# The S5 scan's tile laid out by place in eight instead of chunk by chunk

## The chip, the cores and the metric

The kernel runs on one core of a Trainium2 chip. The metric is the device time of one execution in microseconds; the median of several executions counts. Beside it stands one execution recorded by the hardware profiler, from which all durations below are read. TensorE is called PE there, VectorE DVE, ScalarE ACT, GpSimd POOL, and SyncE, which issues most DMAs, SP.

## The reference, cut to what matters

One layer of a streaming encoder: two groups of heads side by side, latent attention and a diagonal state-space layer (S5), then a gated convolutional FFN. It is computed for a prompt of 1024 positions and for 8 running streams of 16 positions each. Only the S5 part is touched:

```python
bu_re = jnp.einsum('gpc,bsgc->bsgp', bb_re, ug)      # 32 groups, 64 complex states each
bu_im = jnp.einsum('gpc,bsgc->bsgp', bb_im, ug)
ar, ai, sr, si = lax.associative_scan(comb, (la_re, la_im, bu_re, bu_im), axis=1)
if h0_re is not None:                                 # running streams: carried state
    h_re, h_im = h0_re[:, None], h0_im[:, None]
    sr, si = sr + ar * h_re - ai * h_im, si + ar * h_im + ai * h_re
y = (jnp.einsum('gcp,bsgp->bsgc', p["s5_c_re"], sr)
     - jnp.einsum('gcp,bsgp->bsgc', p["s5_c_im"], si))
```

That is a linear recurrence s(t) = a s(t-1) + B u(t) for each of 32 x 64 complex states, and an output read from each state. Its last states are outputs too.

## The kernel before

All three phases of the kernel work on 1152 positions: 1024 of the prompt and 128 of the streams. `phase_a` norms and projects the input: first the S5 channels (`upart`), then for each 128 positions the query and kv latents (`natpart`, matmuls into `nat`). `phase_b` does the attention of the streams and the S5 layer, `phase_de` drives the prompt's attention (`phase_c`), the output projection and the FFN, which is most of the time.

The S5 layer cuts positions into chunks of 8 (`LC`), so there are 144 chunks (`NCH`): 128 of the prompt (`NPC`), then two for each of the 8 streams. `tables` computes powers of a and three sets of matrices: `Et` (from a chunk's input to its contribution to the state), `f_dram` (from a state to a chunk's outputs) and `kt_dram` (within a chunk). The last two are made by the generator `rest` in eight rounds, each with three VectorE operations of 128x576 (`tmpF`, `fo`), eight matmuls `kp`, a ScalarE copy into `kts`, one small VectorE addition and two stores.

`s5_states` (L424) computes each chunk's contribution: 32 groups, three to a PSUM bank `pst`, one matmul each (128 partitions: 64 real parts, 64 imaginary parts). ScalarE copies the real half into `RE` (L435), VectorE the imaginary half into `IM` (L436). Both are halves of the tile `RI`, [128, 2, 16, 144]: the partition is (half of the groups, state), then real or imaginary, then 16 groups, then the 144 chunks in order.

`s5_scan` (L438) makes of these the state at each chunk's end. The 128 chunks of the prompt are read as 16 blocks b of 8 places i, chunk = 8 b + i.
- Local steps, L474: for i = 1 to 7, `cmac2` adds a times place i-1 to place i, in all 16 blocks and 16 groups at once. One `cmac2` (L387) is five VectorE operations: a product of 512 elements, two of 256 with the other part and a sign, and two sums of 512. The works `v1` and `v2` (shown as `w`) are whole runs; the operands in `RI` step 8 elements, 32 bytes, within a group.
- Across blocks, L477 to 489: the last place of each block (`SL`) goes into `SB`, where small operations carry the states through four quarters (`SC`).
- Fix-up, L498 to 511: each block's places 0 to 6 get a's power times the state before the block, by `cmac` (L403: eight VectorE operations), four blocks at a time, 448 elements an operation. After each, ScalarE copies the states into `SP`, shifted by one chunk, for the output matmul: for each of real and imaginary and each half of the groups one copy of 64x448 and one of 64x64 from `SB`, 32 in all.
- Streams, L512 to 526: two `cmac` of 128 elements with the carried state `h0`, copies into `SP`, and the last states into `fin`.

`SP` is [128, 32, 144] in the order of chunks, since `s5_out` (L529) multiplies it and `U`, the input in chunks, by `Ft` and `Tt` into `py`.

`b8_open` and `b8_q` prepare the attention of the streams: loads of `cq`, `wq`, `wk`, `wkT` and small vectors, transposes `tq` with ScalarE copies `cqT`, projections, their sums of squares, and from them the factors `rrq`, `ex`; `b0` in `phase_b` goes on from there (`qah`, `qal`).

The order of the code is not the order on the chip. L1722 opens the tile context with `schedule_with_timeline_sim=True`: a planner orders each engine's instructions, SyncE's DMAs among them, by its own estimate of when each can start, apart from the stretches with a manual order (L1593). So the scan's steps, called in `phase_b` by `steps`, stand on VectorE between the work of `rest` and of `natpart`. Within an engine instructions run in the planned order. `GD` and `GF` are 16, so `cmac` and `cmac2` run on VectorE alone.

Of the kernel before, what the change touches and what calls it, by code (L numbers as in the profile page):

```python
# [75 lines left out]
def build(tc, t):  # L76
# [4 lines left out]
    with root:  # L81
# [19 lines left out]
        def acopy(out, in_, scale=1.0):  # L101
            nc.scalar.activation(out=out, in_=in_, func=AF.Copy, scale=scale)  # L102
# [321 lines left out]
        def s5_states():  # L424
            RI, h0, Et, U = [s5t[x] for x in ("RI", "h0", "Et", "U")]
            RE, IM = RI[:, 0], RI[:, 1]
            load(h0, t["h0"])
            for gh in range(2):
                for q0 in range(0, 16, 3):
                    n = min(3, 16 - q0)  # L430
                    p_ = psum("u", [P, n, NCH], "pst")
                    for g in range(n):
                        gg_ = gh * 16 + q0 + g
                        nc.tensor.matmul(p_[:, g], lhsT=Et[:, gg_], rhs=U[:, gg_], start=True, stop=True)
                    acopy(RE[64 * gh:64 * gh + 64, q0:q0 + n], p_[0:64])  # L435
                    nc.vector.tensor_copy(out=IM[64 * gh:64 * gh + 64, q0:q0 + n], in_=p_[64:P])  # L436

        def s5_scan():  # L438
            RI, SG, w1, PWr, PWi, SB, h0, fin, SC, QWr, QWi = [s5t[x] for x in (
                "RI", "SG", "w1", "PWr", "PWi", "SB", "h0", "fin", "SC", "QWr", "QWi")]  # L440
            RE, IM, SBr, SBi = RI[:, 0], RI[:, 1], SB[:, 0], SB[:, 1]
            nc.vector.tensor_copy(out=PWr[:, :, 0], in_=LRc)
            nc.vector.tensor_copy(out=PWi[:, :, 0], in_=LIc)

            def powers(xr, xi, n):
                d = 1
                while d < n:
                    ar, ai = xr[:, :, 0:d], xi[:, :, 0:d]
                    br = xr[:, :, d - 1:d].to_broadcast([P, 16, d])
                    bi = xi[:, :, d - 1:d].to_broadcast([P, 16, d])  # L450
                    orr, oi = xr[:, :, d:2 * d], xi[:, :, d:2 * d]
                    w = w1[:, :, 0:d]
                    mul(orr, ar, br)
                    mul(w, ai, bi)
                    sub(orr, orr, w)
                    mul(oi, ar, bi)
                    mul(w, ai, br)
                    add(oi, oi, w)
                    d *= 2

            powers(PWr, PWi, LC)
            nc.vector.tensor_copy(out=QWr[:, :, 0], in_=PWr[:, :, LC - 1])
            nc.vector.tensor_copy(out=QWi[:, :, 0], in_=PWi[:, :, LC - 1])
            powers(QWr, QWi, 4)
            for k, z in enumerate((PWi[:, :, 0], QWi[:, :, 0], QWi[:, :, 3])):
                ts(SG[:, k, 0], z, -1.0, None, ALU.mult)
                nc.vector.tensor_copy(out=SG[:, k, 1], in_=z)
            nc.vector.memset(SB[:, :, :, 0:1], 0.0)
            nc.vector.memset(SC[:, :, :, 0:1], 0.0)
            yield  # L470
            RP = RE[:, :, 0:NPC].rearrange("p g (b i) -> p g b i", i=LC)
            IP = IM[:, :, 0:NPC].rearrange("p g (b i) -> p g b i", i=LC)
            RIp = RI[:, :, :, 0:NPC].rearrange("p r g (b i) -> p r g b i", i=LC)
            for i in range(1, LC):  # L474
                cmac2(RIp[:, :, :, :, i], RIp[:, :, :, :, i - 1], RIp[:, :, :, :, i], 0, 16, GD)
                yield
            SL = RIp[:, :, :, :, LC - 1].rearrange("p r g (q n) -> p r g q n", n=4)  # L477
            SQ = SB[:, :, :, 1:17].rearrange("p r g (q n) -> p r g q n", n=4)
            nc.vector.tensor_copy(out=SQ[:, :, :, :, 0], in_=SL[:, :, :, :, 0])
            for i in range(1, 4):  # L480
                cmac2(SQ[:, :, :, :, i], SQ[:, :, :, :, i - 1], SL[:, :, :, :, i], 1, 4, 16)
            yield
            for q in range(4):
                cmac2(SC[:, :, :, q + 1:q + 2], SC[:, :, :, q:q + 1], SQ[:, :, :, q:q + 1, 3], 2, 1, 16)
            yield
            nc.vector.tensor_copy(out=SQ[:, :, :, :, 3], in_=SC[:, :, :, 1:5])
            qr, qi = [x[:, :, 0:3].rearrange("p g (o i) -> p g o i", o=1).to_broadcast([P, 16, 3, 3]) for x in (QWr, QWi)]
            cr_, ci_ = [SC[:, r, :, 1:4].rearrange("p g (b o) -> p g b o", o=1).to_broadcast([P, 16, 3, 3]) for r in range(2)]
            cmac(SQ[:, 0, :, 1:4, 0:3], SQ[:, 1, :, 1:4, 0:3], qr, qi, cr_, ci_, gd=16)
            yield  # L490
            SP = s5t["SP"] = s5t["pool"].tile([P, G, NCH], F32, tag="ES", name="SP")

            def sp_views(ri, gh):
                si = slice(64 * gh, 64 * gh + 64)
                o = SP[64 * ri:64 * ri + 64, 16 * gh:16 * gh + 16]
                return si, o[:, :, 0:NPC].rearrange("p g (b i) -> p g b i", i=LC), o[:, :, NPC:NCH].rearrange("p g (b i) -> p g b i", i=2)

            n7 = LC - 1  # L498
            pr = PWr[:, :, 0:n7].rearrange("p g (o i) -> p g o i", o=1).to_broadcast([P, 16, 4, n7])
            pi = PWi[:, :, 0:n7].rearrange("p g (o i) -> p g o i", o=1).to_broadcast([P, 16, 4, n7])  # L500
            for b0_ in range(0, 16, 4):
                bs_ = slice(b0_, b0_ + 4)
                br = SBr[:, :, bs_].rearrange("p g (b o) -> p g b o", o=1).to_broadcast([P, 16, 4, n7])
                bi = SBi[:, :, bs_].rearrange("p g (b o) -> p g b o", o=1).to_broadcast([P, 16, 4, n7])
                cmac(RP[:, :, bs_, 0:n7], IP[:, :, bs_, 0:n7], pr, pi, br, bi, gd=GF)
                for ri in range(2):
                    for gh in range(2):
                        si, ov, _ = sp_views(ri, gh)
                        acopy(ov[:, :, bs_, 1:LC], (RP, IP)[ri][si, :, bs_, 0:LC - 1])
                        acopy(ov[:, :, bs_, 0], SB[si, ri, :, bs_])  # L510
                yield
            RS = RE[:, :, NPC:NCH].rearrange("p g (b i) -> p g b i", i=2)  # L512
            IS = IM[:, :, NPC:NCH].rearrange("p g (b i) -> p g b i", i=2)
            m8r = PWr[:, :, 0:1].to_broadcast([P, 16, NB])
            m8i = PWi[:, :, 0:1].to_broadcast([P, 16, NB])
            cmac(RS[:, :, :, 0], IS[:, :, :, 0], m8r, m8i, h0[:, 0], h0[:, 1])
            cmac(fin[:, 0, :, 1:], fin[:, 1, :, 1:], m8r, m8i, RS[:, :, :, 0], IS[:, :, :, 0],
                 RS[:, :, :, 1], IS[:, :, :, 1])
            for ri in range(2):
                for gh in range(2):  # L520
                    si, _, os_ = sp_views(ri, gh)
                    acopy(os_[:, :, :, 0], h0[si, ri])
                    acopy(os_[:, :, :, 1], (RS, IS)[ri][si, :, :, 0])
            nc.vector.tensor_copy(out=fin[:, 0, :, 0], in_=SBr[:, :, 16])
            nc.vector.tensor_copy(out=fin[:, 1, :, 0], in_=SBi[:, :, 16])
            store(t["s5"], fin)
            yield
# [1216 lines left out]
```

## Time and profile before

| what | us |
|---|---|
| median of 3 runs | 1547.39 (1546.98 to 1550.94) |
| the profiled execution's own time | 1547.78 |
| its span, from the first to the last instruction | 1546.0 |
| TensorE busy | 1470.7 |
| VectorE busy | 1101.9 |
| ScalarE busy | 692.8 |

The S5 states are copied between 110.9 and 125.9 us, the scan runs from 125.9 to 226.7 us; all that is later than some 280 us has nothing of the change in it. A line of the timeline gives start, length, engine, line, operation and what it writes and reads, and in brackets the idle time of the engine before it and who ended it. A line of the groups gives the count, the busy time of all and the mean of one in ns. L105 is the line of a helper, so many groups have it; the tile names tell them apart.

### The profile page before, as it was taken

The page shows a single profiled execution, that of the slowest core. Times are in us where ns is not written, and L with a number is a line of the kernel's source. Part 1 is how long each engine was busy: PE and PEld are TensorE (multiplying, and loading weights), DVE is VectorE, ACT ScalarE, POOL GpSimd, SP SyncE. Part 2 cuts the span into 40 slices and gives each one's busy share as a digit, 9 for nine tenths or more (in the row PEclk, how much of TensorE's full clock was granted, in tenths as well). Part 3 has the DMA queues.
Part 4 walks back from the last instruction along what each step waited for, and adds up shares of the span by engine and source line. Part 5 has one row for each costly group of instructions (what it writes and reads, how often), then busy time and mean ns, then how long its engine had stood idle before and what let it go on. Part 6 is the DMA issues. An engine that isn't in the chain of part 4 may idle for free.

```text
span 1546.0 us, 23671 instructions
## 1 busy us (share of the span) xinstructions
PE 1470.7 (95%) x8733; PEld 1416.0 (92%) x8733; DVE 1101.9 (71%) x2317; ACT 692.8 (45%) x1351; POOL 261.8 (17%) x517
## 2 busy tenths in 40 slices
PE   6989759899899999999999999999999999999998
PEld 6988548787788999999999999999999999999998
DVE  8779986573878865567677766677777766777666
ACT  7444557575567876345233333333333333333321
POOL 3025222210635221112100000000000000000000
PEclk9999869999899999999999999999999999999999
DMA  7432553733211323630121111111111111111103
GB/s 204 113 128 74 167 154 70 233 78 97 79 58 58 103 67 101 199 88 15 41 68 43 42 44 48 47 41 42 42 42 41 42 42 42 42 42 42 42 1 133
DMA packets 92036, 117.95 MB, mean 76 GB/s; under 512 B 39060, under 2 KB 72980, under 8 KB 91188
## 3 DMA queue, kind: packets, MB, share of 16 engines
q1 hardware_dynamic: 91536, 116.25, 25.3%
q8 instruction: 68, 1.11, 0.3%
q14 instruction: 48, 0.39, 0.1%
q0 software_dynamic: 384, 0.20, 0.1%
HBM read 91.86 MB, written 24.56 MB: 75 GB/s over the span
## 4 chain that ended last, share of the span: by engine, by line
PE 77%; DVE 8%; ACT 2%; DMA 2%; issue 1%; SPq 0%; POOL 0%; DVEq 0%; ACTq 0%
PE pu L138 36%; PE pd L138 17%; PE pw L138 7%; PE pk L138 3%; PE pg L138 1%; DVE w L105 1%; PE pq L138 1%; PE po L1273 1%; PE pst L1261 1%; PE pst L1260 1%; PE pst L1262 1%; PE po L1271 1%; PE po L1272 1%; PE pZ L1032 1%; PE psm L1228 1%
## 5 line engine op out<-in xcount | busy, mean ns | idle before, releaser
L105 DVE TENSOR_TENSOR hT<-hT,pd 128x384 f32<-128x384 f32 x528 | 288.2, 551 | 217.6 <-PE pd L138 217.4
L138 PE MATMUL pu<-hnh,wh 128*128 128x384 f32 x1056 | 356.6, 338 | 0.0
L138 PE MATMUL pu<-hnl,wh 128*128 128x384 f32 x1056 | 356.4, 338 | 0.0
L138 PE MATMUL pu<-hnh,wl 128*128 128x384 f32 x1056 | 356.1, 337 | 0.0
L138 PE MATMUL pd<-act,wh 128*128 128x384 f32 x1056 | 348.7, 336 | 0.5 <-DVE hT L105 0.4
L1543 ACT ACTIVATE c<-pu,cvh 128x384 f32<-128x384 f32 x132 | 88.6, 671 | 308.8 <-PE pu L138 308.6
L138 PEld LDWEIGHTS pd<-act,wh 128*128 128x128 f32 x1056 | 197.7, 188 | 2.3 <-DVE hT L105 2.3
L138 PEld LDWEIGHTS pu<-hnh,wh 128*128 128x128 f32 x1056 | 198.4, 188 | 0.0
L138 PEld LDWEIGHTS pu<-hnl,wh 128*128 128x128 f32 x1056 | 198.3, 188 | 0.0
L138 PEld LDWEIGHTS pu<-hnh,wl 128*128 128x128 f32 x1056 | 198.0, 188 | 0.0
L123 DVE SCALAR_TENSOR_TENSOR c<-u,cvh,c 128x256 f32<-128x256 f32 (+1 forms) x352 | 171.2, 516 | 27.5 <-ACT u L102 14.2
L138 PE MATMUL pd<-act,wl 128*128 128x384 f32 x528 | 177.4, 336 | 0.0
L102 ACT ACTIVATE act<-c 128x384 fp32r<-128x384 f32 x66 | 34.7, 525 | 158.2 <-DVE c L105 158.2
L138 PEld LDWEIGHTS pd<-act,wl 128*128 128x128 f32 x528 | 99.2, 188 | 0.0
L105 DVE TENSOR_TENSOR wl<-ws,wh 128x1024 fp32r<-128x1024 f32 x74 | 92.0, 1248 | 8.0 <-ACT wh L102 8.0
L1549 POOL COPY u<-u 128x2 f32<-128x2 f32 x88 | 19.8, 225 | 384.3 <-DVE c L105 174.0
L102 ACT ACTIVATE wh<-ws 128x1024 fp32r<-128x1024 f32 x74 | 77.9, 1057 | 13.6 <-PE pw L138 7.5
L1565 ACT ACTIVATE c<-c 128x384 f32<-128x384 f32 x66 | 34.7, 525 | 75.5 <-DVE c L123 75.4
L1561 POOL COPY cvo<-u 128x2 f32<-128x2 f32 x44 | 8.1, 184 | 356.1 <-ACT u L102 356.1
L102 ACT ACTIVATE u<-pu 128x384 f32<-128x384 f32 (+2 forms) x176 | 66.3, 404 | 0.0
L138 PE MATMUL pw<-oh,wh 128*128 128x384 f32 x192 | 65.1, 340 | 0.2 <-DVE ql L123 0.2
L138 PE MATMUL pw<-oh,wl 128*128 128x384 f32 x192 | 64.4, 336 | 0.0
(450 smaller groups left out, 3043.1 us busy)
## 6 DMA issues: line engine op xcount, KB each, us to landing
ws<-in_w_up SPq DMA_DIRECT2D x44, 512.0 KB, 3.5
ws<-in_w_down SPq DMA_DIRECT2D x22, 512.0 KB, 3.6
xs<-in_xT SPq DMA_DIRECT2D x24, 192.0 KB, 3.0
os<-o_dram SPq DMA_DIRECT2D x24, 192.0 KB, 2.8
hT<-in_xT SPq DMA_DIRECT2D x24, 192.0 KB, 4.6
out_yT<-hT SPq DMA_DIRECT2D x24, 192.0 KB, 2.2
cf<-in_cT SPq DMA_DIRECT2D x8, 512.0 KB, 4.1
cn<-in_cn SPq DMA_DIRECT2D x8, 512.0 KB, 4.8
```

What stands on the lines that cost most here:

```text
L102: nc.scalar.activation(out=out, in_=in_, func=AF.Copy, scale=scale)
L105: (eng or nc.vector).tensor_tensor(out=out, in0=a, in1=b, op=op)
L123: nc.vector.scalar_tensor_tensor(out=out, in0=a, scalar=s, in1=b, op0=op0, op1=op1)
L138: nc.tensor.matmul(out, lhsT=w, rhs=x, start=first and i == 0, stop=last and i == n - 1)
L1032: nc.tensor.matmul(p_, lhsT=PT[:, c], rhs=cn[:, c] if c < 4 else c8n, start=c == 0, stop=c == 4)
L1228: nc.tensor.matmul(p_[:, u, 0:n], lhsT=qh[0:r, h, z * P:(z + 1) * P], rhs=kT[jj][0][0:r, 4 * g + h, 0:n], start=True, stop=True)
L1260: nc.tensor.matmul(o_, lhsT=kh[0:r, 4 * g + h, ks], rhs=qh[0:r, h, qs_], start=True, stop=False)
L1261: nc.tensor.matmul(o_, lhsT=kl[:, 4 * g + h, ks], rhs=qh[0:QD, h, qs_], start=False, stop=False)
L1262: nc.tensor.matmul(o_, lhsT=kh[0:QD, 4 * g + h, ks], rhs=ql[:, h, qs_], start=False, stop=True)
L1543: nc.scalar.activation(out=c, in_=p_, func=AF.Identity, scale=w[2], bias=w[3])
L1549: nc.gpsimd.tensor_copy(out=u[:, 0:2], in_=halo[i, gv][:, TB:TB + 2])
L1565: nc.scalar.activation(out=g_, in_=g_, func=AF.Silu)
```

## The change

`RI` keeps its size, but its 144 chunks stand as (place i in eight, block b of eighteen): chunk 8 b + i is element 18 i + b. The sixteen blocks of the prompt at one place are now neighbours; blocks 16 and 17 are the streams' chunks.

- `s5_states`: the copies out of PSUM read `pst` in steps of 8 elements and write `RI` in runs of 18.
- Local steps: `RIp` is a view by places; the five operations and their sizes are the same, with runs of 16.
- Fix-up: two places at a time for all 16 blocks, 512 elements an operation, and one place in the last of four rounds. Its copies into `SP` write in steps of 8 elements: per round four of 64x512 (64x256 in the last), and in the first round four of 64x256 from the whole of `SB`; 20 in all.
- Streams: `RS`, `IS`, `h0` and `fin` are viewed to match; `RS` and `IS` are runs of one with steps of 36 elements and of one.

```diff
-                    acopy(RE[64 * gh:64 * gh + 64, q0:q0 + n], p_[0:64])
-                    nc.vector.tensor_copy(out=IM[64 * gh:64 * gh + 64, q0:q0 + n], in_=p_[64:P])
+                    pv = p_.rearrange("p g (b i) -> p g i b", i=LC)
+                    re_, im_ = [x[64 * gh:64 * gh + 64, q0:q0 + n].rearrange("p g (i b) -> p g i b", i=LC) for x in (RE, IM)]
+                    acopy(re_, pv[0:64])
+                    nc.vector.tensor_copy(out=im_, in_=pv[64:P])
...
-            RP = RE[:, :, 0:NPC].rearrange("p g (b i) -> p g b i", i=LC)
-            IP = IM[:, :, 0:NPC].rearrange("p g (b i) -> p g b i", i=LC)
-            RIp = RI[:, :, :, 0:NPC].rearrange("p r g (b i) -> p r g b i", i=LC)
+            RP = RE.rearrange("p g (i b) -> p g i b", i=LC)[:, :, :, 0:16]
+            IP = IM.rearrange("p g (i b) -> p g i b", i=LC)[:, :, :, 0:16]
+            RIp = RI.rearrange("p r g (i b) -> p r g i b", i=LC)[:, :, :, :, 0:16]
             for i in range(1, LC):
-                cmac2(RIp[:, :, :, :, i], RIp[:, :, :, :, i - 1], RIp[:, :, :, :, i], 0, 16, GD)
+                cmac2(RIp[:, :, :, i], RIp[:, :, :, i - 1], RIp[:, :, :, i], 0, 16, GD)
                 yield
-            SL = RIp[:, :, :, :, LC - 1].rearrange("p r g (q n) -> p r g q n", n=4)
+            SL = RIp[:, :, :, LC - 1].rearrange("p r g (q n) -> p r g q n", n=4)
...
-            for b0_ in range(0, 16, 4):
-                bs_ = slice(b0_, b0_ + 4)
-                br = SBr[:, :, bs_].rearrange("p g (b o) -> p g b o", o=1).to_broadcast([P, 16, 4, n7])
-                bi = SBi[:, :, bs_].rearrange("p g (b o) -> p g b o", o=1).to_broadcast([P, 16, 4, n7])
-                cmac(RP[:, :, bs_, 0:n7], IP[:, :, bs_, 0:n7], pr, pi, br, bi, gd=GF)
+            for i0 in range(0, n7, 2):
+                ni = min(2, n7 - i0)
+                is_ = slice(i0, i0 + ni)
+                pr, pi = [x[:, :, is_].rearrange("p g (i o) -> p g i o", o=1).to_broadcast([P, 16, ni, 16]) for x in (PWr, PWi)]
+                br, bi = [x[:, :, 0:16].rearrange("p g (o b) -> p g o b", o=1).to_broadcast([P, 16, ni, 16]) for x in (SBr, SBi)]
+                cmac(RP[:, :, is_], IP[:, :, is_], pr, pi, br, bi, gd=GF)
                 for ri in range(2):
                     for gh in range(2):
                         si, ov, _ = sp_views(ri, gh)
-                        acopy(ov[:, :, bs_, 1:LC], (RP, IP)[ri][si, :, bs_, 0:LC - 1])
-                        acopy(ov[:, :, bs_, 0], SB[si, ri, :, bs_])
+                        ovi = ov.rearrange("p g b i -> p g i b")
+                        acopy(ovi[:, :, i0 + 1:i0 + 1 + ni], (RP, IP)[ri][si, :, is_])
+                        if i0 == 0:
+                            acopy(ov[:, :, :, 0], SB[si, ri, :, 0:16])
                 yield
...
-            RS = RE[:, :, NPC:NCH].rearrange("p g (b i) -> p g b i", i=2)
-            IS = IM[:, :, NPC:NCH].rearrange("p g (b i) -> p g b i", i=2)
+            RS, IS = [x.rearrange("p g (s h b) -> p g b s h", h=2, b=18)[:, :, 16:18] for x in (RE, IM)]
...
-            cmac(RS[:, :, :, 0], IS[:, :, :, 0], m8r, m8i, h0[:, 0], h0[:, 1])
+            cmac(RS[:, :, :, :, 0], IS[:, :, :, :, 0], m8r, m8i, hr, hi_)
```

## Rows read from the trace of the kernel before

**Rows 1.** The page: engines with busy time and share; shares of the last chain.

```profile
PE 1470.7 (95%) x8733; PEld 1416.0 (92%) x8733; DVE 1101.9 (71%) x2317; ACT 692.8 (45%) x1351; POOL 261.8 (17%) x517
...
PE 77%; DVE 8%; ACT 2%; DMA 2%; issue 1%; SPq 0%; POOL 0%; DVEq 0%; ACTq 0%
```

**Rows 2.** Stretches: busy us of PE, PEld, DVE, ACT, POOL; clock, DMA share, GB/s.

```profile
111.30:126.00 14.70, 14.70 (x106) 13.51 (x106) 13.78 (x46) 9.78 (x26) 0.59 (x3) 1.00 0.24 74
126.00:176.30 50.30, 46.04 (x290) 42.52 (x288) 50.13 (x123) 18.89 (x49) 29.04 (x20) 0.97 0.24 75
176.30:190.00 13.70, 7.16 (x17) 3.91 (x17) 10.43 (x42) 10.29 (x31) 0.93 (x4) 0.75 0.97 277
190.00:206.70 16.70, 2.31 (x6) 0.68 (x4) 16.70 (x30) 8.04 (x16) 7.29 (x4) 0.66 0.58 196
```

**Rows 3.** Timeline of PE, the longest stop before 176 us.

```profile
160.94 1.68 PE L348 MATMUL kp<-fo,bb 128*16 128x128 f32 x8 [2.02 <-DVE kts L105]
```

**Rows 4.** Timeline of ACT, DVE and SP: projection 4 and the load behind it.

```profile
169.46 0.48 ACT L102 ACTIVATE nat<-nat,rx 128x288 f32<-128x288 f32 x1
...
170.51 0.29 ACT L155 ACTIVATE rsw<-sq,epsc 128x2 f32<-128x2 f32 x1
...
172.49 0.16 DVE L120 TENSOR_SCALAR rsv<-sq 128x2 f32<-128x2 f32 x1
...
174.99 0.62 ACT L102 ACTIVATE nat<-nat,rq 128x384 f32<-128x384 f32 x1
...
175.63 0.34 SPq L99 DMA_DIRECT2D cq_dram<-nat  x1
...
177.44 0.45 SPq L96 DMA_DIRECT2D cq<-cq_dram  x1
```

**Rows 5.** Timeline of PE and DVE: the waits behind the loads.

```profile
180.09 0.30 PE L585 MATMUL tq<-ident,cq 128*128 128x128 f32 x1 [3.70 <-DMA cq<-cq_dram]
...
189.46 0.15 DVE L123 SCALAR_TENSOR_TENSOR gq<-gq,gk 96x1 f32<-96x1 f32 x1 [1.24 <-DMA gk<-in_g_kh]
...
206.96 0.48 PE L621 MATMUL rk<-ident,ex 128*128 128x128 f32 x1 [14.64 <-DVE ex L619]
```

**Rows 6.** Groups by shape up to 420 us: the operations of the local steps.

```profile
L105 DVE TENSOR_TENSOR w<-RI,SG 128x256 f32<-128x256 f32 x14 | 8.6, 634 | 0.0
L105 DVE TENSOR_TENSOR w<-w,RI 128x512 f32<-128x512 f32 x7 | 8.0, 1143 | 0.0
L105 DVE TENSOR_TENSOR w<-RI,PWr 128x512 f32<-128x512 f32 x7 | 7.9, 1128 | 0.0
```

**Rows 7.** The same view: operations with whole runs (runs of seven in the second).

```profile
L105 DVE TENSOR_TENSOR epre<-LRr,bb 128x512 f32<-128x512 f32 x8 | 5.4, 685 | 2.7 <-PE ep L326 2.6
...
L105 DVE TENSOR_TENSOR w<-w,w 128x448 f32<-128x448 f32 x8 | 4.9, 615 | 0.0
...
L105 DVE TENSOR_TENSOR cTl<-ct,cTh 128x256 fp32r<-128x256 f32 x5 | 2.1, 417 | 1.7 <-ACT cTh L102 1.7
```

**Rows 8.** The copies out of PSUM: two groups, and one line of DVE's timeline.

```profile
L436 DVE COPY RI<-pst 64x432 f32<-64x432 f32 x10 | 6.0, 610 | 4.4 <-PE pst L434 3.7 <-ACT RI L102 0.5
...
L102 ACT ACTIVATE RI<-pst 64x432 f32<-64x432 f32 x10 | 5.0, 520 | 3.7 <-PE pst L434 3.7
...
117.23 0.61 DVE L436 COPY RI<-pst 64x432 f32<-64x432 f32 x1 [0.51 <-ACT RI L102]
```

**Rows 9.** Groups of ACT up to 420 us: copies with and without steps.

```profile
L102 ACT ACTIVATE gh<-gf 128x384 fp32r<-128x384 f32 x12 | 10.3, 887 | 4.7 <-DMA gf<-y_dram 4.7
L102 ACT ACTIVATE SP<-RI 64x448 f32<-64x448 f32 x16 | 9.2, 573 | 0.4 <-DVE RI L105 0.2
...
L102 ACT ACTIVATE SP<-SB 64x64 f32<-64x64 f32 x16 | 5.1, 318 | 2.4 <-DVE rq L156 2.2
...
L102 ACT ACTIVATE qrh<-qrs 32x128 fp32r<-32x128 f32 x8 | 2.4, 306 | 0.2
L102 ACT ACTIVATE wgh<-wg 128x512 fp32r<-128x512 f32 x4 | 2.4, 629 | 0.0
```

More of the change, by code (lines that the diff above doesn't have):

```diff
@@ L498, in s5_scan @@
             n7 = LC - 1
-            pr = PWr[:, :, 0:n7].rearrange("p g (o i) -> p g o i", o=1).to_broadcast([P, 16, 4, n7])
-            pi = PWi[:, :, 0:n7].rearrange("p g (o i) -> p g o i", o=1).to_broadcast([P, 16, 4, n7])
-            for b0_ in range(0, 16, 4):
-                bs_ = slice(b0_, b0_ + 4)
-                br = SBr[:, :, bs_].rearrange("p g (b o) -> p g b o", o=1).to_broadcast([P, 16, 4, n7])
-                bi = SBi[:, :, bs_].rearrange("p g (b o) -> p g b o", o=1).to_broadcast([P, 16, 4, n7])
-                cmac(RP[:, :, bs_, 0:n7], IP[:, :, bs_, 0:n7], pr, pi, br, bi, gd=GF)
+            for i0 in range(0, n7, 2):
[4 more added lines that the diff above has]
+                cmac(RP[:, :, is_], IP[:, :, is_], pr, pi, br, bi, gd=GF)
                 for ri in range(2):
@@ L508, in s5_scan @@
                         si, ov, _ = sp_views(ri, gh)
-                        acopy(ov[:, :, bs_, 1:LC], (RP, IP)[ri][si, :, bs_, 0:LC - 1])
-                        acopy(ov[:, :, bs_, 0], SB[si, ri, :, bs_])
+                        ovi = ov.rearrange("p g b i -> p g i b")
+                        acopy(ovi[:, :, i0 + 1:i0 + 1 + ni], (RP, IP)[ri][si, :, is_])
+                        if i0 == 0:
+                            acopy(ov[:, :, :, 0], SB[si, ri, :, 0:16])
                 yield
-            RS = RE[:, :, NPC:NCH].rearrange("p g (b i) -> p g b i", i=2)
-            IS = IM[:, :, NPC:NCH].rearrange("p g (b i) -> p g b i", i=2)
-            m8r = PWr[:, :, 0:1].to_broadcast([P, 16, NB])
-            m8i = PWi[:, :, 0:1].to_broadcast([P, 16, NB])
-            cmac(RS[:, :, :, 0], IS[:, :, :, 0], m8r, m8i, h0[:, 0], h0[:, 1])
-            cmac(fin[:, 0, :, 1:], fin[:, 1, :, 1:], m8r, m8i, RS[:, :, :, 0], IS[:, :, :, 0],
-                 RS[:, :, :, 1], IS[:, :, :, 1])
+            RS, IS = [x.rearrange("p g (s h b) -> p g b s h", h=2, b=18)[:, :, 16:18] for x in (RE, IM)]
+            m8r, m8i = [x[:, :, 0:1].rearrange("p g (o u) -> p g o u", u=1).to_broadcast([P, 16, 2, 4]) for x in (PWr, PWi)]
+            hr, hi_ = [h0[:, z].rearrange("p g (b s) -> p g b s", s=4) for z in range(2)]
+            fr_, fi_ = [fin[:, z, :, 1:].rearrange("p g (b s) -> p g b s", s=4) for z in range(2)]
+            cmac(RS[:, :, :, :, 0], IS[:, :, :, :, 0], m8r, m8i, hr, hi_)
+            cmac(fr_, fi_, m8r, m8i, RS[:, :, :, :, 0], IS[:, :, :, :, 0],
+                 RS[:, :, :, :, 1], IS[:, :, :, :, 1])
             for ri in range(2):
@@ L522, in s5_scan @@
                     acopy(os_[:, :, :, 0], h0[si, ri])
-                    acopy(os_[:, :, :, 1], (RS, IS)[ri][si, :, :, 0])
+                    acopy(os_[:, :, :, 1].rearrange("p g (b s) -> p g b s", s=4), (RS, IS)[ri][si, :, :, :, 0])
             nc.vector.tensor_copy(out=fin[:, 0, :, 0], in_=SBr[:, :, 16])
```

## The prediction

> **What bounds the kernel now.** I read the page first: TensorE is busy for 95% of the span and carries 77% of the chain that ended last, VectorE carries 8% [rows 1]. An average of 95% can't say what a VectorE edit at the front is worth, so the second view is the busy time by stretch [rows 2]. From 111.3 to 126.0 us TensorE never stops and VectorE has 0.9 us to spare. From 126.0 to 176.3 us the order is turned round: VectorE works 50.13 of 50.30 us, TensorE 46.04. This is the stretch in which the seven local steps of the scan run, mixed by the planner with the S5 tables and the projections `nat`. After it come the loads of the next part (176.3 to 190), a stretch where VectorE has no free moment (16.70 of 16.70) while TensorE stands nearly still, and then TensorE's long work, which ends the kernel. So the front is a series of handovers, and a microsecond won there is won at the end only if it passes all of them.
>
> The third view shows the handovers. TensorE's 4.3 us of stops inside the second stretch are four, and the longest, 2.02 us, ends on VectorE's `kts` [rows 3]. The last one that matters is not TensorE's: projection 4 was read out of PSUM at 169.46, but its five small VectorE instructions ran from 172.49 on, between scan work, the ScalarE one after them at 174.99, its store was issued at 175.63, and only behind it and three more stores SyncE issued the load of `cq`, at 177.44 [rows 4]. TensorE waits for that `cq` until 180.09, VectorE waits at 189.46 for a load issued in the same row of loads, and TensorE then stands 14.64 us until VectorE has made `ex` [rows 5]. The scan feeds none of these; it only stands in their way on VectorE.
>
> **The change part by part.** *The steps.* Each of seven steps has three operations of 128x512 and two of 128x256 whose scan operand steps 32 bytes: 1.128 and 1.143 us (the third kind, the write, has 1.128 again), and 0.634 us [rows 6]. Three whole-run operations give the price without that: 0.685 us at 512, 0.615 at 448 (there in runs of seven), 0.417 at 256 [rows 7]. Runs of sixteen should be no dearer than runs of seven. A step thus saves 0.443 + 0.458 + 0.443 + 2 x 0.217 = 1.78 us, seven save 12.4 us of VectorE time. The three `SL` reads keep a step of 16 bytes: nothing.
>
> *The fix-up.* Four groups of 8 x 448 become three of 8 x 512 and one of 8 x 256: 32 x 0.615 = 19.7 us before, 24 x 0.685 + 8 x 0.417 = 19.8 after. Nothing. The sample part is new in one point: eight 128x128 operands now step 144 bytes. At the surplus of the steps, (1.128 - 0.685) / 512 = 0.87 ns an element, that is 0.9 us; part of it lies between other VectorE work, I take 0.5 (0 to 0.9).
>
> *The copies out of PSUM.* Twelve on VectorE (0.610 us each, two are a third as long) and twelve on ScalarE (0.520) now read PSUM in steps of 32 bytes [rows 8]. No row shows such a read. Below zero is excluded, since today's reads and writes are already whole runs. The ends are nothing and the surplus of the SBUF rows: 0.87 x 432 = 0.38 us for a VectorE copy, 4.0 us for 10.7 full ones, and 4.4 us on ScalarE at the 0.95 ns found below. I take the upper end, because every row with such a step pays, on both engines; both ends stay in the range. VectorE hardly has cover for it (0.9 us), so the 4.0 us stay as a backlog at 126 us, and TensorE may stand for PSUM buffers; I take 1.5 us of that (0 to 4.0).
>
> The Trainium skill, page "PSUM — Partial Sum Buffer", section "Specifications (TRN2)", gives PSUM lines of 8 bytes and says that non-contiguous patterns slow matmuls much; for reads by the other engines it states nothing and no row here shows one. By that rule, carried over to them, the copies would pay, which speaks against the change; if they don't pay, the sum below is 7.0 us and not 5.5, and VectorE's lead is 4.0 us longer.
>
> *The copies into `SP`.* ScalarE wrote sixteen of 64x448 at 0.573 and sixteen of 64x64 at 0.318, 14.3 us. Now it writes in steps of 32 bytes: twelve of 512 elements, four of 256, and four of 256 from `SB`. ScalarE's price without steps is 0.306 us at 128 and 0.629 at 512 elements, so 0.521 at 384; a stepped read of 384 took 0.887, a surplus of 0.95 ns an element [rows 9]. That gives 1.115 us at 512 and 0.657 at 256, in all 13.4 + 5.3 = 18.6 us, 4.3 more. From 176.3 to 206.7 us ScalarE is busy for 18.3 of 30.4 us [rows 2], but `cqT` and `qah`, which TensorE and VectorE wait for, queue behind these copies; I take 1.0 us on the path (0 to 4.3). The first `SB` copies could start before `SB` was whole; now all wait for it. `SP`'s readers come behind the loads of `Tt`, so that costs nothing unless the planner puts a waiting copy in front of something.
>
> *The sum.* VectorE's load in the second stretch falls from 50.1 to 50.1 - 12.4 + 4.0 = 41.7 us, under TensorE's 46.0. TensorE becomes the bound and the stretch shrinks by 50.3 - 46.0 = 4.3 us, less the 1.5 us of PSUM stalls. Then the lag of projection 4: from its read-out's end (169.9) to its store (175.63) pass 5.7 us, of which its own instructions are 0.9 on ScalarE (to the root's end, 170.80), five of 0.16 on VectorE and 0.62 on ScalarE [rows 4]: 2.3, with gaps some 2.5. A VectorE with room gives back 3.2 us (0 to 3.4). So the loads start 4.3 - 1.5 + 3.2 = 6.0 us earlier, and VectorE's own queue is 8.4 us earlier: 2.4 us of fix-up can run before the loads land and not in the full stretch behind them, if the planner orders it so; I take 1.0 (0 to 4.9). Sum: 6.0 + 1.0 - 1.0 (ScalarE) - 0.5 (sample) = 5.5 us. From the profiled execution's 1547.78 us (span 1546.0 and 1.8 around it) that is 1542.3; the median of the runs lies 0.4 lower, so **1541.9**.
>
> **The rivals.** *One: VectorE's time passes whole.* If the PSUM read costs nothing and the planner uses VectorE's lead for the fix-up, all 12.4 us less the 1.5 of ScalarE and sample arrive: 1547.4 - 10.9 = 1536.5. For it: VectorE is the full engine in two of the three front stretches. Against it: TensorE has only 4.3 us to give in the first, and the loads cost what they cost.
>
> *Two: no change.* TensorE stands the full 4.0 us for PSUM buffers, ScalarE's copies cost 2.3 us before `ex`, the sample part 0.9: 4.3 - 4.0 + 3.2 - 2.3 - 0.9 = 0.3, so 1547.1. For it: the twelve pairs lie where VectorE has 0.9 us free, and one bank is read by ScalarE and then VectorE, one after the other (VectorE waited 0.51 for that at 117.23 [rows 8]).
>
> *Three: slower, by the PSUM reads.* If a stepped PSUM read is far dearer than an SBUF one, the cost moves from the scan to the copies. Break-even is a surplus of 12.4 / 10.7 = 1.16 us a VectorE copy (1.77 instead of 0.61); from there VectorE still bounds the second stretch and ScalarE's share comes on top. At 1.5 us: 16.0 - 12.4 + 2.2 (half of ScalarE's 4.3) = 5.8 slower, 1553.2. For it: the row that would exclude it is missing. Against it: no stepped row here costs more than twice its whole-run price.
>
> That the steps don't get faster is hardly open: runs of seven elements already cost 1.37 ns each against 1.34 for one run.
>
> **How the numbers follow.** About 0.3%, 4.6 us, is what a measurement of this kernel can tell from no change: below 1542.75 is faster, above 1552.0 slower. Forecast (1539.5 to 1545.5) 0.45, of which 0.34 lies below 1542.75 and 0.11 above, since the centre is within a microsecond of that mark. Rival one 0.18, two 0.24, three 0.13. Faster 0.34 + 0.18 = 0.52, same 0.11 + 0.24 = 0.35, slower 0.13. The range goes from near rival one's best (12.4 less: 1535.0) to the worst of the bounded terms (4.3 - 4.0 - 4.3 - 0.9 = 4.9 lost: 1552.3), each end drawn in a little: 1535.5 to 1551.5.
>
> **What would show it.** Step operations at 0.69 and 0.42 us, else the first term is wrong. The copies out of PSUM at 0.99 (VectorE) and 0.93 (ScalarE): at 0.61 and 0.52 rival one gains, above 1.7 rival three. In the stretch of the projections TensorE without gaps and VectorE with some. The load of `cq` issued near 171.5 us and not 177.4. ScalarE's `SP` copies at 1.1 us. `ex` ready near 201. What would make it wrong: the planner, which orders every queue anew from its own times, may put scan work before the small instructions of the projections, or `SP` copies before `cqT`; then the lag stays though VectorE has room.

## The result, and the profile after

The kernel after takes **1530.71 us** (median of 4 runs, 1529.24 to 1532.97) against 1547.18 in the same comparison: a ratio of 0.9894, 95% interval 0.9875 to 0.9913, so 16.5 us faster. In three later comparisons it took 1530.38, 1530.62 and 1529.77. The forecast was 1541.9 with a range from 1535.5 to 1551.5: the right sign, a third of the size, and outside the range.

The profiled execution took 1530.32 us, with a span of 1528.5. Engines with busy time and share, of the kernel after (of before: [rows 1]):

```profile
PE 1463.4 (96%) x8733; PEld 1409.1 (92%) x8733; DVE 1087.5 (71%) x2317; ACT 694.3 (45%) x1337; POOL 250.9 (16%) x517
```

VectorE is busy 14.4 us less than before, TensorE 7.3 us less. TensorE has the same 8733 matmuls, so those 7.3 us fit a change of its granted clock (on average 0.976 before, 0.981 after); the other 10.2 of the 17.5 us of span are time in which it stood.

Three stretches of the front of after, from the end of the states' copies to `rk` (columns as in [rows 2], which has the same three parts at 126.0 to 206.7):

```profile
126.00:171.00 45.00, 45.00 (x298) 42.18 (x296) 42.74 (x146) 19.04 (x50) 14.88 (x20) 1.00 0.32 98
171.00:185.00 14.00, 7.25 (x19) 3.74 (x18) 10.87 (x27) 11.70 (x21) 1.91 (x4) 0.88 0.97 276
185.00:199.20 14.20, 2.75 (x4) 0.70 (x4) 14.20 (x24) 10.71 (x15) 6.01 (x4) 0.55 0.48 180
```

The first is what the forecast wanted: TensorE without a gap, VectorE with 2.3 us to spare. In the last one VectorE is still full (14.20 of 14.20), as before.

VectorE's groups by shape from 126 to 230 us, kernel after (of before: [rows 6, 7]):

```profile
L105 DVE TENSOR_TENSOR w<-PWr,SB 128x512 f32<-128x512 f32 x6 | 5.6, 941 | 0.0
L105 DVE TENSOR_TENSOR w<-RI,SG 128x256 f32<-128x256 f32 x14 | 5.6, 416 | 0.0
...
L105 DVE TENSOR_TENSOR w<-w,RI 128x512 f32<-128x512 f32 x7 | 4.7, 671 | 0.0
L105 DVE TENSOR_TENSOR w<-PWi,SB 128x512 f32<-128x512 f32 x6 | 4.1, 682 | 0.0
```

The steps cost 0.416 and 0.67 us instead of 0.634 and 1.13 to 1.14. One fix-up operation of six lies at 2.24 us, as one of before's does at 2.22; the others take 0.68.

ScalarE's copies from 111 to 230 us, and VectorE's copies out of PSUM (in the last the durations are minimum, median and maximum in ns), kernel after (of before: [rows 8, 9]):

```profile
L102 ACT ACTIVATE SP<-RI 64x512 f32<-64x512 f32 x12 | 13.6, 1132 | 3.4 <-DVE RI L105 3.3
L102 ACT ACTIVATE RI<-pst 64x432 f32<-64x432 f32 x10 | 5.0, 521 | 3.7 <-PE pst L434 3.6
...
L102 ACT ACTIVATE SP<-SB 64x256 f32<-64x256 f32 x4 | 2.6, 655 | 0.0
```

```profile
L438 DVE COPY RI<-pst x12: 302/609/611, 112.6 to 126.7; 64x432 f32<-64x432 f32 x10, 64x144 f32<-64x144 f32 x2
```

The copies that now read PSUM in steps of 32 bytes take what they took: 609 ns after 610 on VectorE, 521 after 520 on ScalarE. `SP`'s stepped writes cost 1.132 and 0.655 us.

**The way through the kernel by four marks.** The next rows are TensorE's tiles `pst` (states), `nat` (projections), `rk` (end of the front) and `pw` (output projection); before the semicolon stands the start of the first and the last matmul. Kernel before:

```profile
L434 PE MATMUL pst<-U,Et x64: 283/286/448, 88.9 to 123.1; 128*128 128x144 f32 x64
...
L138 PE MATMUL nat<-wnh,xlo x144: 289/334/522, 73.8 to 176.0; 128*128 128x384 f32 x72, 128*128 128x288 f32 x72
...
L621 PE MATMUL rk<-ident,ex x1: 476/476/476, 207.0 to 207.0; 128*128 128x128 f32 x1
...
L138 PE MATMUL pw<-oh,wh x192: 331/336/443, 568.3 to 705.5; 128*128 128x384 f32 x192
```

Kernel after:

```profile
L434 PE MATMUL pst<-U,Et x64: 283/286/448, 89.9 to 124.2; 128*128 128x144 f32 x64
...
L138 PE MATMUL nat<-wnh,xlo x144: 290/331/472, 75.0 to 170.8; 128*128 128x384 f32 x72, 128*128 128x288 f32 x72
...
L624 PE MATMUL rk<-ident,ex x1: 474/474/474, 199.5 to 199.5; 128*128 128x128 f32 x1
...
L138 PE MATMUL pw<-oh,wh x192: 331/336/448, 550.8 to 688.0; 128*128 128x384 f32 x192
```

From the last `pst` to the last `nat`: 52.9 us before, 46.6 after. From there to `rk`: 31.0 and 28.7. From `rk` to the first `pw`: **361.3 and 351.3**. From there on nothing differs (977.7 us to the end in both). The first mark itself lies 1.1 us later in this execution of after. So 6.3 + 2.3 + 10.0 - 1.1 = 17.5 us, and more than half of it arises behind `rk`, where only the end of the change's own work is left (the scan's last operations run until 219 us, before until 227).

### The profile page after: what moved, and what is told of

Read it like the earlier page. It is cut to its first block, busy times and chain, and to the rows that moved or that the text cites. A ratio compares the mean times of both kernels' runs of the same rounds, so it can differ in the third digit from the quotient of the medians.

```text
span 1528.5 us, 23656 instructions
## 1 busy us (share of the span) xinstructions
PE 1463.4 (96%) x8733; PEld 1409.1 (92%) x8733; DVE 1087.5 (71%) x2317; ACT 694.3 (45%) x1337; POOL 250.9 (16%) x517
## 4 chain that ended last, share of the span: by engine, by line
PE 81%; DVE 8%; DMA 4%; ACT 3%; issue 2%; POOL 1%; SPq 0%; DVEq 0%; ACTq 0%; POOLq 0%
PE pu L138 36%; PE pd L138 17%; PE pw L138 7%; PE nat L138 3%; PE pk L138 2%; DMA ws<-in_w_in 1%; PE pq L138 1%; PE up L138 1%; PE po L1276 1%; PE pst L1263 1%; PE pst L1264 1%; PE pS L138 1%; PE po L1274 1%; PE pst L1265 1%; PE po L1275 1%
## 5 line engine op out<-in xcount | busy, mean ns | idle before, releaser
L138 PE MATMUL pu<-hnh,wl 128*128 128x384 f32 x1056 | 356.1, 337 | 0.0
```

The lines of the kernel that those rows point to most:

```text
L138: nc.tensor.matmul(out, lhsT=w, rhs=x, start=first and i == 0, stop=last and i == n - 1)
```

## The experiments

All times are medians in us, ratios are against the kernel before on the same chip, with 95% intervals. The theory after the first result: two gains, one of the steps in the front, one of another order of the streams' attention. Its rival: the order doesn't matter, and shorter operations in the front carry everything. In the expectations of the first two experiments the theory is called B and the rival A, in those of the reordered kernels the theory is A and the rival B.

**Which part brings it.** Steps alone: new layout, states, steps and streams' part (the forecast's sample part), with the fix-up and its 32 copies in four groups of four blocks as before. Against the kernel after:

```diff
-            for i0 in range(0, n7, 2):
-                ni = min(2, n7 - i0)
...
-                cmac(RP[:, :, is_], IP[:, :, is_], pr, pi, br, bi, gd=GF)
+            for b0_ in range(0, 16, 4):
+                bs_ = slice(b0_, b0_ + 4)
...
+                cmac(RP[:, :, 0:n7, bs_], IP[:, :, 0:n7, bs_], pr, pi, br, bi, gd=GF)
...
+                        acopy(ovi[:, :, 1:LC, bs_], (RP, IP)[ri][si, :, 0:n7, bs_])
+                        acopy(ov[:, :, bs_, 0], SB[si, ri, :, bs_])
```

> The new layout with the states' copies and the local steps of the change, but the fix-up as before in four groups of four blocks (448 elements an operation, now in runs of four) and 32 copies into SP. The planner gives every engine the order of the kernel before, so this is the price of the cheaper steps alone, in the old order. Theory A (all of the gain is VectorE time of the steps): 1531 to 1535 us, near the changed kernel. Theory B (the front gives 6 to 8 us, the rest is the new order of the streams' attention): 1539 to 1542 us. Forecast's terms unchanged: a gain of 5.5 to 7, since the reads of PSUM cost nothing. In all cases: step operations 0.67 and 0.41 us; load of cq issued some 8 us earlier than 177.4.

1539.81 (1531.27 to 1540.67), ratio 0.9939 [0.9920, 0.9958]: 8.5 us, half of the gain. Every engine's instructions stand in the order of the kernel before, although the steps have become 40% shorter. So the planner's order did not follow what the steps cost, and what this kernel gains is the durations' alone. One of its six executions took 1531.27, at a granted clock of 0.985 where the others had 0.975 to 0.981; its trace isn't kept. A single execution can't tell two orders apart, a median can.

Fix-up alone: the layout and steps of before, but the fix-up two places at a time, with 20 copies. Against the kernel before:

```diff
-            for b0_ in range(0, 16, 4):
...
-                cmac(RP[:, :, bs_, 0:n7], IP[:, :, bs_, 0:n7], pr, pi, br, bi, gd=GF)
+            RPi, IPi = [x.rearrange("p g b i -> p g i b") for x in (RP, IP)]
+            for i0 in range(0, n7, 2):
...
+                cmac(RPi[:, :, is_], IPi[:, :, is_], pr, pi, br, bi, gd=GF)
```

> The layout of before, so the local steps keep their 32-byte steps at 1.13 us, but the fix-up goes by places as in the change (512 elements an operation, stepped here, 20 copies into SP). The planner gives every engine the order of the changed kernel. Theory A: no gain, 1546 to 1551 us (the fix-up's sums are stepped, some 3 us of VectorE more). Theory B: the new order keeps its part, 1537 to 1542 us. If the two parts help each other, both this and the run with the steps alone lie nearer to the kernel before than their sum says.

1541.60 (1539.75 to 1546.34), ratio 0.9960 [0.9945, 0.9975]: faster too, although its fix-up now steps 32 bytes and costs VectorE more, as its groups from 170 to 230 us show (the kernel after takes 0.674 us for this one):

```profile
L105 DVE TENSOR_TENSOR RI<-w,RI 128x512 f32<-128x512 f32 x6 | 6.5, 1083 | 0.0
```

It has TensorE's order of the kernel after, instruction for instruction. A fix-up that costs more and a gain behind it: what is left for the gain is the order. The kernel after beside them:

> The changed kernel itself beside the others on the same chip, as the fourth corner of the two parts: 1530.7 us and a ratio of 0.989.

1530.38, ratio 0.9891 [0.9875, 0.9907].

**The stepped writes of `SP`.** `SP` laid out by places, so that ScalarE writes whole runs and TensorE reads in steps of 18 elements. Against the kernel after:

```diff
-                        acopy(ovi[:, :, i0 + 1:i0 + 1 + ni], (RP, IP)[ri][si, :, is_])
+                        acopy(ov[:, :, i0 + 1:i0 + 1 + ni], (RP, IP)[ri][si, :, is_])
...
-                                     rhs=SP[:, g0 + g], start=False, stop=True)
+                                     rhs=SP[:, g0 + g].rearrange("p (i b) -> p b i", i=LC), start=False, stop=True)
```

> The changed kernel with SP laid out by places too: ScalarE's 16 copies of the states and 4 of SB write whole runs, and TensorE reads SP in steps of 18 elements for the output matmul. Same order on every engine as the changed kernel. ScalarE's copies from 1.12 to about 0.63 us, 18.5 to about 10.5 us in all. If the copies lie on the path as the forecast's 1.0 us: 1529 to 1530. If ScalarE is as much in the way as its 1.4 us waits before ssqq and cqT look: 1526 to 1528. If TensorE pays for stepped reads (64 matmuls of 0.286 us): slower by up to 64 x 0.2 = 13 us, 1535 to 1544.

1538.61 (1535.87 to 1542.97), ratio 0.9943 [0.9927, 0.9960], 8 us over the kernel after. ScalarE's copies fell to 0.643 us for 512 elements and 0.411 for the 256 from `SB`, but TensorE's 64 matmuls on `SP`, here and then in the kernel after:

```profile
L546 PE MATMUL py<-SP,Ft x64: 402/414/425, 231.2 to 283.9; 128*128 128x144 f32 x64
```

```profile
L547 PE MATMUL py<-SP,Ft x64: 285/286/288, 231.0 to 276.2; 128*128 128x144 f32 x64
```

64 x 0.128 = 8.2 us on TensorE, which is the bound there: the price of the step is better paid by ScalarE.

**The same work in another order.** The decisive pair. The fix-up takes 7 places, two at a time and one at the end. Where the single place stands changes no operation's size or number on TensorE and VectorE, but it changes the planner's order. With 1, 2, 2, 2 TensorE's order is that of the kernel before in all but ten of 8733 places; with 2, 1, 2, 2 it is a third one. Both against the kernel after:

```diff
-            for i0 in range(0, n7, 2):
-                ni = min(2, n7 - i0)
+            for i0, ni in ((0, 1), (1, 2), (3, 2), (5, 2)):
```

> The kernel after with its seven places of the fix-up taken as 1, 2, 2, 2 and not as 2, 2, 2, 1: same layout, same 24 operations of 512 and 8 of 256 elements, the same 20 copies into SP. Only the small round stands first. With that the planner orders the streams' attention on TensorE as it did in the kernel before. Theory A (two gains: about 8 us from the steps, which pass through the front, and about 9 us from another order of the streams' attention): the second gain goes, 1538 to 1541 us, ratio 0.993 to 0.996, with TensorE idle for some 23 us between 230 and 600 us instead of 15.6, its wait for ex in the streams at 3.6 us and not 1.0. Rival B (the order doesn't matter; whole-run operands and fewer, larger copies give all 17.5 us): 1530 to 1532 us, ratio 0.989 to 0.990.

**1542.85** (1540.16 to 1546.37), ratio 0.9969 [0.9958, 0.9980]; a little over the upper end of what theory A gave, and far from the rival's. The wait for `ex` is at 3.6 us, TensorE's idle time from 230 to 600 us at 24.6.

```diff
-            for i0 in range(0, n7, 2):
-                ni = min(2, n7 - i0)
+            for i0, ni in ((0, 2), (2, 1), (3, 2), (5, 2)):
```

> The same again with the places taken as 2, 1, 2, 2. The planner makes a third order of the streams' attention of it, neither that of the kernel before nor that of after. Theory A (the order decides about 9 us, and nothing in the change aims at it): between 1525 and 1542 us, and the distance to the kernel after is the difference of TensorE's idle time between 230 and 600 us, with what the clock loses in it, to within 3 us. Rival B (the order doesn't matter): 1530 to 1532 us.

1530.56 (1529.80 to 1532.74), ratio 0.9894 [0.9875, 0.9912]: the third order is as good as that of after.

The kernel before with one edit, sixteen copies from `SB` joined to four, which gives it the third order too (but for one matmul):

```diff
-                        acopy(ov[:, :, bs_, 0], SB[si, ri, :, bs_])
+                        if b0_ == 0:
+                            acopy(ov[:, :, :, 0], SB[si, ri, :, 0:16])
```

> The kernel before, with its layout, its stepped scan and its four fix-up groups of 448 elements; only the sixteen copies of 64x64 from SB into SP become four of 64x256 in the first group. VectorE does exactly the work of before, ScalarE some 2.5 us less. The planner's order becomes the third one. Theory A: the time moves by the order's worth alone, and by the same amount, to within 3 us, as the 2, 1, 2, 2 kernel differs from the 1, 2, 2, 2 one. Rival B: 1545 to 1548 us, ratio 0.998 to 1.000.

1535.86 (1531.97 to 1540.07), ratio 0.9921 [0.9902, 0.9940]. That is **11.4 us for the old layout with VectorE's work untouched**, beside 12.3 us between the 1, 2, 2, 2 and the 2, 1, 2, 2 kernel. The rival had given 1545 to 1548.

> The kernel after on the same chip, to be compared with the others of this call. Theory A and rival B: 1529 to 1532 us, ratio 0.988 to 0.991.

1530.62, ratio 0.9891 [0.9872, 0.9911].

The stretch from 230 to 600 us in five kernels (columns as in [rows 2]): before, 1, 2, 2, 2, after, 2, 1, 2, 2, and the old layout with joined copies.

```profile
230.00:600.00 370.00, 347.44 (x2309) 312.95 (x2308) 261.21 (x594) 252.91 (x475) 112.03 (x176) 0.96 0.33 93
```

```profile
230.00:600.00 370.00, 345.40 (x2324) 311.86 (x2323) 258.35 (x592) 252.74 (x475) 110.62 (x177) 0.97 0.32 94
```

```profile
230.00:600.00 370.00, 354.43 (x2424) 322.28 (x2423) 260.55 (x596) 255.85 (x487) 115.85 (x178) 0.99 0.31 96
```

```profile
230.00:600.00 370.00, 353.19 (x2430) 321.19 (x2429) 259.56 (x598) 256.76 (x489) 117.65 (x178) 0.99 0.32 97
```

```profile
230.00:600.00 370.00, 352.18 (x2404) 318.78 (x2404) 260.61 (x599) 256.21 (x486) 116.04 (x177) 0.99 0.33 96
```

TensorE stands for 22.6 and 24.6 us of the 370 in the order of before, 15.6 in that of after, 16.8 and 17.8 in the third, and the granted clock is 0.96 to 0.97 in the first two, 0.99 in the others. But these windows don't hold the same work, since `rk` lies at another time in each.

A fairer piece goes from the 300th matmul after `rk` to the 1000th. These 700 are the same in all kernels and come in three orders; the scan is done by then, and of the change only TensorE's reads of `SP` reach into it. Before, after and the fix-up alone (the counts take in two matmuls at the edges):

```profile
266.24:408.64 142.40, 129.89 (x702) 111.44 (x701) 88.23 (x208) 88.35 (x158) 31.54 (x58) 0.95 0.42 125
```

```profile
263.86:392.03 128.17, 122.65 (x702) 106.45 (x701) 84.62 (x203) 84.03 (x157) 31.38 (x55) 1.00 0.45 137
```

```profile
277.42:407.89 130.47, 125.03 (x702) 108.58 (x701) 83.01 (x203) 84.13 (x157) 31.50 (x55) 0.97 0.44 135
```

Here the order of after takes 14.2 us less than that of before. 7.0 of them are stops (12.5 and 5.5 us), the other 7.2 are busy time of the same matmuls, at a granted clock of 1.00 and not 0.95. In the 300 matmuls ahead of this piece the new order wins nothing: they take 59.3 us before and 64.3 after.

What TensorE waited for from 230 to 600 us (in total, times, longest), in the 1, 2, 2, 2 kernel and in the kernel after; `pRK` and `pZ` belong to the streams' attention, `pg` to the S5 gate, `ex` and `U` are made by VectorE and ScalarE:

```profile
PE pRK L998 <- DVE ex L990: 3.6, 1, 3.6
PE pg L138 <- ACT gh L102: 3.0, 2, 1.7
PE py L545 <- DMA Tt<-kt_dram: 2.7, 1, 2.7
...
PE pk L138 <- ACT U L548: 2.2, 1, 2.2
PE pZ L1034 <- ACT PT L102: 1.8, 1, 1.8
```

```profile
PE pk L138 <- ACT sq L985: 2.6, 1, 2.6
...
PE pRK L999 <- DVE ex L991: 1.0, 1, 1.0
PE pg L138 <- ACT gh L102: 0.9, 1, 0.9
...
PE pZ L1035 <- ACT PT L102: 0.3, 1, 0.3
```

No single wait carries it. In the order of before TensorE meets `ex`, `gh`, `U` and `PT` too early; in that of after these shrink and one for `sq` comes up. In the third order, which is as good, `ex` is waited for 3.7 us.

The wait for `U` can be followed to its cause. ScalarE makes the last piece of `U` with a GELU, and an exponential of the attention (L1010, in after L1013) stands beside it. Kernel before, then after:

```profile
279.94 1.28 ACT L1010 ACT_TABLE_LOAD   x1 [0.79 <-DVE nm L1009]
...
282.08 1.28 ACT L546 ACT_TABLE_LOAD   x1
283.37 0.41 ACT L546 ACTIVATE U<-py 128x288 f32<-128x288 f32 x1
```

```profile
276.48 0.41 ACT L549 ACTIVATE U<-py 128x288 f32<-128x288 f32 x1 [0.69 <-PE py L547]
...
278.82 1.28 ACT L1013 ACT_TABLE_LOAD   x1
```

In the order of before the exponential goes first, with a table load of 1.28 us ahead of each of the two; in the other orders `U` goes first and has none. TensorE waits 2.2 us for this `U` in all five traces with the order of before and in none of the others. In all, ScalarE loads a table 23 times in the order of before and 21 times in the two others, so the twin's work differs by two such loads.

The wait for `Tt` is of another kind, SyncE's row of DMA issues, the 1, 2, 2, 2 kernel first, then the kernel after:

```profile
220.91 0.35 SPq L99 DMA_DIRECT2D out_s<-fin  x1
221.36 10.75 SPq L96 DMA_DIRECT2D Tt<-kt_dram  x8
```

```profile
216.25 1.69 SPq L96 DMA_DIRECT2D Tt<-kt_dram  x3
219.05 0.35 SPq L99 DMA_DIRECT2D out_s<-fin  x1
```

Here the store of `fin`, made last by the scan, stands in front of all of `Tt`'s loads; there three go ahead of it. `Tt`'s first load starts at 221.36 and not 216.25, which is 1.5 us later when measured from `rk`. It is no mark of the worse order: the stop is 0.6 us in the later trace of the same kernel, and in the third order the store stands in front too.

**Do the two add up?** The steps-only kernel with joined copies, which has steps, old groups and the third order. Against the steps-only kernel:

```diff
-                        acopy(ov[:, :, bs_, 0], SB[si, ri, :, bs_])
+                        if b0_ == 0:
+                            acopy(ov[:, :, :, 0], SB[si, ri, :, 0:16])
```

> The new layout with its states and steps, the fix-up four blocks at a time as in the kernel before (448 elements), and the copies from SB joined to four of 64x256 in the first group. It is the steps-only kernel with that one edit, and the planner gives it the third order of the streams' attention. Theory A (steps and order add up): the joined copies bring here what they brought to the kernel before (11.4 us), so 1539.8 - 11.4 = 1528.4, between 1525 and 1531 us, ratio 0.986 to 0.990, at or a little below the kernel after. Rival B (the order's gain and the steps' gain are the same stall, taken away once): 1533 to 1536 us, no better than the old layout with joined copies.

1530.56 (1528.54 to 1532.94), ratio 0.9908 [0.9891, 0.9926]: within theory A's time, just outside its ratio, and no faster than the kernel after, which took 1529.77 on the same chip:

> The kernel after on the same chip, for the three others. All theories: 1529.5 to 1531.5 us, ratio 0.988 to 0.991.

The steps-only and the 1, 2, 2, 2 kernel side by side:

> The steps-only kernel once more, beside the 1, 2, 2, 2 kernel: both have the order of before on TensorE and the same steps, they differ only in how the fix-up and its copies are grouped. Theory A (grouping by places has a small price of its own, ScalarE's stepped writes and the sample part): 1538 to 1541 us, 1.5 to 4 us under the 1, 2, 2, 2 kernel. Rival B (no price of its own): the two within 1 us.

> The 1, 2, 2, 2 kernel once more, on the same chip as the steps-only kernel and the kernel after. Theory A: 1541 to 1544 us, 10 to 13 us over the kernel after, whose work it has in the order of before. Rival B of the run before: 1539 to 1541 us.

1539.56 (ratio 0.9963 [0.9950, 0.9977]) and 1542.32 (0.9976 [0.9961, 0.9990]; kernel after on this chip 0.9907 [0.9889, 0.9925]): with the order held, grouping by places with the joined copies costs 2.8 us, and what comes with the other order brings 12.6. Joining the copies brings the steps-only kernel 9.0 us here (1539.56 to 1530.56), beside 11.4 in the old layout, so the two gains add up but for some 2 us.

The marks of all kernels, worked out from the tile views as above; `cq` load is the start of `cq`'s load on SyncE, and the last column is the piece of 700 matmuls.

| kernel | order | last `pst` to last `nat` | last `pst` to `cq` load | `cq` load to `rk` | `rk` to first `pw` | 300th to 1000th matmul after `rk` |
|---|---|---|---|---|---|---|
| before | before's | 52.9 | 54.3 | 29.5 | 361.3 | 142.4 |
| steps alone (twice) | before's | 46.5, 46.6 | 44.7, 44.7 | 29.3, 29.5 | 360.7, 361.2 | 143.0, 140.7 |
| 1, 2, 2, 2 (twice) | before's | 46.5, 46.6 | 44.6, 44.6 | 32.4, 32.9 | 360.7, 360.7 | 140.9, 142.4 |
| after (four) | after's | 46.5 to 46.6 | 44.6 to 44.7 | 30.1 to 31.6 | 348.2 to 351.7 | 128.2 to 128.7 |
| 2, 1, 2, 2 | third | 46.6 | 44.6 | 30.2 | 352.3 | 130.2 |
| old layout, joined copies | third | 52.9 | 54.0 | 29.9 | 347.9 | 130.1 |
| steps, joined copies | third | 46.6 | 44.7 | 31.9 | 352.1 | 130.4 |
| fix-up alone | after's | 54.5 | 54.0 | 31.5 | 356.1 | 130.5 |
| `SP` by places | after's | 46.6 | 44.6 | 32.3 | 361.6 | 133.5 |

The first two columns follow the layout, the last one the order; `SP` by places has 32 of its dearer matmuls in that piece, 4.1 us. The column before it follows the order with more scatter, since it also holds the end of the scan and the clock there. The fix-up alone is off in that column and in the first. Its trace is of an execution 4.7 us over the kernel's median, 1546.34, with a clock of 0.89 from 230 to 280 us where the kernel after has 1.00. From the 1000th matmul on all kernels have the same order.

## Why the prediction was wrong, point by point

**Right.** The steps: 0.67 and 0.416 us against the forecast's 0.685 and 0.417, so 12.7 us of VectorE time where 12.4 stood. TensorE without a gap in the stretch of the projections. `SP`'s copies: 1.132 and 0.655 to 0.689 against 1.115 and 0.657. The fix-up: no cheaper, no dearer on VectorE. The shape of the front: VectorE's gain is cut off by TensorE and by the loads.

**Mis-sized: the stops for PSUM (-1.5).** They don't exist. The stepped read of PSUM, taken at 0.38 us a copy because every stepped row of SBUF pays, costs nothing on either engine. The forecast had kept nothing as the other end. The Trainium skill, page "SBUF — State Buffer", section "Door 1: The DMA port swizzle (why `[64,N]` ≈ `[32,N]`)", says that accesses are fast as long as two of them fall into one line of 16 bytes, and gives PSUM lines of 8 bytes, with a warning for matmuls only. For the SBUF operands here that agrees (1.13 us in steps of 32 bytes, 0.67 in runs); carried over, as the forecast did, to reads of PSUM by VectorE and ScalarE it doesn't (609 ns after 610, 521 after 520).

**Mis-sized: TensorE's stops (+4.3).** The stretch shrank by 6.3 us. 4.3 are the stops. Most of the rest is the clock behind them; two stretches of the kernel before (columns as in [rows 2]):

```profile
150.00:160.00 10.00, 8.10 (x53) 7.52 (x53) 10.00 (x19) 3.50 (x9) 9.41 (x6) 1.00 0.24 75
160.00:170.00 10.00, 8.74 (x49) 7.75 (x50) 10.00 (x21) 2.77 (x7) 0.87 (x2) 0.83 0.21 60
```

Behind the stop of 2.02 us, which ends at 160.94 [rows 3], the granted clock is 0.83, a mean of the levels 2.4 and 1.2 GHz; in the kernel after it is 1.00 through the whole stretch. Ten microseconds at 0.83 are 1.7 us. The forecast counted a stop only by its length.

**Mis-sized: the lag of projection 4 (+3.2).** Timeline of ScalarE and SyncE, kernel after (of before: [rows 4]):

```profile
162.72 0.50 ACT L102 ACTIVATE nat<-nat,rx 128x288 f32<-128x288 f32 x1 [1.39 <-PE nat L138]
```

```profile
167.05 0.37 SPq L99 DMA_DIRECT2D cq_dram<-nat  x1
...
168.89 0.45 SPq L96 DMA_DIRECT2D cq<-cq_dram  x1
```

From the read-out's end (163.22) to the store (167.05) pass 3.8 us, before 5.7: 1.9 and not 3.2. VectorE has room, but there the planner's order on it is unchanged, so the five small instructions still stand between scan operations. `cq`'s load starts 9.6 us earlier against the last `pst`, where the forecast had 6.0. The read-out itself came 7.8 us earlier (it ends 46.8 and 39.0 us after the last `pst`). Some 5.9 of these are TensorE's, whose last matmul for it ends at 167.42 before and at 162.67 after. The other 2.0 are VectorE's, which the forecast looked for only behind the read-out: before, ScalarE got to it late, since its instruction ahead of it had waited for VectorE.

```profile
168.93 0.62 ACT L102 ACTIVATE nat<-nat,rq 128x384 f32<-128x384 f32 x1 [3.75 <-DVE kts L105]
```

**The price of the new groups (+1.0 - 1.0 - 0.5).** From `cq`'s load to `rk` the kernel after is 0.6 to 2.1 us slower than before, and the 1, 2, 2, 2 kernel 2.9 to 3.4. VectorE's lead, which was to bring the fix-up ahead of the loads, does not cover that. ScalarE's stepped copies and the streams' part, which the forecast priced, don't show as the cause: the steps-only kernels have both (0.98 us for a copy of 64x448 after 0.57) and take 29.3 and 29.5, as before. All kernels with joined copies from `SB` take 29.9 to 32.9. No run parts these copies from both the new groups and the new order, so the cause stays open. The streams' part costs VectorE 0.86 us more (0.9 was the upper end), but it runs behind `rk`, not in the front.

**The failing step: that the sum ends at the front.** The forecast said that the front is a series of handovers and that what passes them arrives at the end. For the front that gave nearly the right net, by errors that cancel: 5.5 us, and with the order held at that of before the change brings 3.6 and 4.4 us (1, 2, 2, 2, both comparisons). What was missing is a term for the order behind the front. That the planner orders every queue anew stood there only as a risk for two places in the front; that a fix-up with other groups and 20 copies instead of 32 would reorder the streams' attention, 60 to 190 us behind `rk`, was not priced at all. The two pairs of medians differ by 12.3 and 12.6 us. In their traces 2.2 and 2.8 of these lie between `cq`'s load and `rk`; the term behind `rk` shows in the 700 matmuls, which take 140.7 to 143.0 us in the order of before and 128.2 to 130.5 in the two others (133.5 with the dearer reads of `SP`). No row of before could give its sign; but a row could give its size: TensorE stood for 22.6 us between 230 and 600 us, and what another order can win is bounded by such stops and the clock behind them. What it can lose no row bounds. The range should have reached at least some 10 us to both sides for that.

So the change is two things. Its work, done in a given order, is worth 4 to 5 us (4.4 and 3.6 in the order of before, 5.3 in the third), the steps alone 8.5 and 6.4. The other 12 us came by chance, with an order that nothing in the change aimed at; an equally good one comes to the old layout from joining sixteen copies to four. None of the versions tried beats the kernel after; two equal it.

What stays open: why the planner's first difference in the fix-up's groups turns into a better order behind `rk`, which of its stops hang on ScalarE's two table loads beyond the one for `U`, and whether an order with fewer stops than 15 us exists.

## What to carry to other kernels

Where a planner orders the instructions, an edit has two effects, the one on durations and the one on the order. Separate them by a neutral twin: the same work, with a group moved, and compare a piece behind the edit that holds the same instructions in both. And price a stop of TensorE at more than its length, since the stretch behind it ran at a lower clock.

## What the runs showed of the hardware

- Reads of PSUM in steps of 32 bytes cost VectorE and ScalarE nothing (609 after 610 ns, 521 after 520 ns for 64x432), while operands in SBUF with the same step cost VectorE 1.13 us instead of 0.67 for 512 elements, and ScalarE's stepped writes of 64x512 1.132 instead of 0.643.
- TensorE's moving operand in SBUF pays as well: 414 ns instead of 286 for 128x144 in steps of 72 bytes.
- After TensorE's stop of 2.02 us the granted clock was 0.83 over the next ten microseconds; without stops it stayed at 1.00 over 45 us.
- An ACT_TABLE_LOAD took ScalarE 1.28 us, and the order of the same operations decided whether 23 or 21 of them ran.
